# A two-layer decoder trunk in split float32 on one core: in W2's half products, the second plain block of the first column moved from ahead of the sixth product to between the second and the fourth

## The chip, the cores and the metric

One NeuronCore of one Trainium2 chip runs the whole kernel. The metric is the device time of one execution in microseconds (us), as the median of several runs. TensorE is called PE (its weight loads PEld), VectorE DVE, ScalarE ACT, GpSimd POOL, and SyncE SP; SP and POOL here mostly issue DMAs.

## The reference

A trunk of two layers over 256 tokens of width 2048: a gated-linear-attention layer, then a layer of sliding-window attention with sinks. Each ends with the MLP that takes most of the time, and that the change is in:

```python
def sqrelu_mlp(h, w1, w2):
    u = jax.nn.relu(h @ w1)        # 256 x 2048 by 2048 x 8192
    return (u * u) @ w2            # 256 x 8192 by 8192 x 2048
...
h = h + sqrelu_mlp(rmsnorm(h, norm_mlp[layer]), mlp_w1[layer], mlp_w2[layer])
```

All is float32.

## The kernel before

**Split float32.** Each float32 operand is held as a rounded high part and a rest (`wh`, `wl` for a weight). A product is then three matmuls: high by high, high by rest, rest by high. Weights come from HBM in blocks of 512 x 512 (a tile of 128 x 4 x 512, 1 MB). `halve` splits a block in two halves: for each, ACT casts 128 x 1024 to `wh` (line 124), then DVE subtracts to get `wl` (line 125). PE uses four slices of 128 rows of a block; each half holds two. There are four half tiles of `wh` in all (two blocks), three of `wl`, and three of `ws`, the tile into which plain blocks are loaded. A tile is refilled only when its last reader is done.

**W2 by sets of half products.** `seven` computes, for two of W2's four columns of 512 and one group g of 2048 of its rows, a 4 x 2 arrangement of blocks: rows 0 and 1 by a Strassen-like scheme of seven products, each for 128 tokens only (12 matmuls of 128 x 512), rows 2 and 3 by plain blocks for all 256 tokens (24 matmuls). Block (i, j) is row i, column j of the two. In each MLP, g goes from 0 to 3, and each g has two sets: n = 0 (columns 0 and 1; the "first set" below) and n = 1 (columns 2 and 3, the "second set"). That is 8 first and 8 second sets. For g over 0 two column pairs of W1 (`two_columns`) are computed ahead of the two sets, so the second sets of g = 0, 1, 2 are followed by W1.

I call the products by the index of their left operand (`op[0]` to `op[6]`); the change's name counts from one. A set runs, in the order of the code: product 0 into PSUM bank A; plain block (2,1) into banks E and F; product 2 into E; plain (3,1) into E and F; product 4 into D; product 6 into C; plain (2,0), then plain (3,0), into A and C; product 5 into D; product 1 into A; product 3 into C. Banks go on accumulating, and DVE reads them between: `x21 += D` after product 4 (line 1163), `x22 -= C` after product 6 (line 1164), `v += D` after product 5, `x11 += A` and `x21 += C` at the end. So a product that goes on in D waits until x21 has read D, and plain (2,0)'s second half, which goes on in C, waits until x22 has read C. `apart=True` puts plain (2,0)'s 12 matmuls for bank A ahead of its 12 for bank C.

**The shared block x.** `x` (tile `wx`) is loaded once a set and then changed in place: POOL's accumulating DMA adds block (0,1) after product 0, DVE adds `y` (tile `wy`, line 1212) after product 4, and block (1,0), called `b21` (lines 1223 to 1225), after product 5. Products 0, 4, 5 and 3 use its states. `b12` is block (0,1) plus y (line 1207), for product 6; the same sum for W1's columns is line 315, and W1's x is line 254 (POOL's accumulating DMA), 256 (its load), 330 (plus y).

**What sets the order.** A scheduler orders each engine's instructions when the program is built. `tc.high_priority(offset=WPRI)` lets loads, splits and sums of weights run ahead of other work. On the chip each engine then takes its own list in order, and waits on semaphores.

Of the kernel before, what the change touches and what calls it, by code (L numbers as in the profile page):

```python
# [21 lines left out]
C = 512  # L22
# [29 lines left out]
def yoco_kernel(ctx: ExitStack, tc: tile.TileContext, x, norms, mlp_w1, mlp_w2, a_w_in, w_glr, w_gate, a_g_o, a_w_o,  # L52
# [24 lines left out]
    def tick():  # L77
        now[0] += 1
        for fn in due.pop(now[0], ()):
            fn()  # L80

    def mm(o, l, r, start=True, stop=True, **kw):
        nc.tensor.matmul(o, lhsT=l, rhs=r, start=start, stop=stop, **kw)  # L83
# [23 lines left out]
    def halve(ws, o=C, n=2, gain=None):  # L107

        whs = [wp.tile([P, 2, C], F32R, name="wh", tag="wh", bufs=WHL) for _ in range(2)]
        wl = wp.tile([P, 4, C], F32R, name="wl", tag="wl", bufs=WS)  # L110
        with tc.high_priority(offset=WPRI):
            for k in range(0, 4, n):
                wh = whs[k // 2]
                js, ks = slice(k % 2, k % 2 + n), slice(k, k + n)
                w = ws[k // 2] if isinstance(ws, list) else ws[:, ks, :o]
                if gain is not None:
                    for j in range(k, k + n):
                        g = gain[:, j:j + 1]
                        h = wh[:, j % 2, :o]
                        nc.scalar.activation(out=h, in_=ws[:, j, :o], func=AF.Copy, scale=g)  # L120
                        nc.vector.scalar_tensor_tensor(out=wl[:, j, :o], in0=ws[:, j, :o], scalar=g, in1=h.bitcast(F32),
                                                       op0=ALU.mult, op1=ALU.subtract)
                    continue
                nc.scalar.copy(out=wh[:, js, :o], in_=w)  # L124
                nc.vector.tensor_sub(out=wl[:, ks, :o], in0=w, in1=wh.bitcast(F32)[:, js, :o])  # L125
        return [(whs[k // 2][:, k % 2], wl[:, k]) for k in range(4)]

    def split_w(parts, step=4, gain=None):
        ws = wp.tile([P, 4, C], F32, name="ws", tag="ws", bufs=WS)
        with tc.high_priority(offset=WPRI):  # L130
            for k in range(0, 4, step):
                ks = slice(k, k + step)
                o = 0
                for ap in parts:
                    n = ap.shape[1]
                    nc.sync.dma_start(out=ws[:, ks, o:o + n],
                                      in_=ap[k * P:(k + step) * P].rearrange("(k p) n -> p k n", p=P))
                    o += n
        return halve(ws, o, min(step, 2), gain)
# [826 lines left out]
    def mlp(w1, w2, act, r, gains):  # L966
# [141 lines left out]
        def seven(w, n, op, us, g, acts, gains, sq, nr):  # L1108
# [6 lines left out]
            def block(i, j):  # L1115
                return w[i * C:(i + 1) * C, (c0 + j) * C:(c0 + j + 1) * C]
# [13 lines left out]
            def use(b):  # L1130
                if b in banks:
                    return banks[b], False
                banks[b] = bank([P, C], "ms" if b in "EF" else "acc")
                return banks[b], True

            def product(b, o, ws):
                p, st = use(b)
                halves = halve(ws)
                for k in range(4):
                    wh, wl = halves[k]  # L1140
                    mm(p, op[o][:, 0, k], wh, st and k == 0, False, skip_group_check=True)
                    mm(p, op[o][:, 0, k], wl, False, False, skip_group_check=True)
                    mm(p, op[o][:, 1, k], wh, False, k == 3, skip_group_check=True)
                tick()
                return p

            def plain(i, j, b0, b1, apart=False):

                halves = split_w([block(i, j)])
                ah, al, _ = us[i]  # L1150
                ps_ = [use(b) for b in (b0, b1)]
                order = [(k, t) for k in range(4) for t in range(NT)]
                for n, (k, t) in enumerate(sorted(order, key=lambda kt: kt[1]) if apart else order):
                    wh, wl = halves[k]
                    p, st = ps_[t]
                    tt = slice(t * P, (t + 1) * P)
                    mm(p, ah[:, k, tt], wh, st and k == 0, False, skip_group_check=True)
                    mm(p, ah[:, k, tt], wl, False, False, skip_group_check=True)
                    mm(p, al[:, k, tt], wh, False, k == 3, skip_group_check=True)
                    if n % 4 == 3:  # L1160
                        tick()
# [48 lines left out]
            sub(x22, product("C", 6, b12))  # L1210
            with tc.high_priority(offset=WPRI):
                nc.vector.tensor_add(out=x, in0=x, in1=y)
            for i in (2, 3):
                plain(i, 0, "A", "C", i == 2)
            p = product("D", 5, x)
            with tc.high_priority(offset=WPRI):
                add(v, p)
# [6 lines left out]
            with tc.high_priority(offset=WPRI):  # L1224
                nc.vector.tensor_add(out=x, in0=x, in1=b21)
            product("A", 1, b21)
            add(x11, banks["A"])
            if g == n + 2 == 3 and not gains:

# [20 lines left out]
        for g in range(4):  # L1250
# [50 lines left out]
            for n in range(2):  # L1301
                seven(w, n, op, us, g, acts, gains, sq, nr)
# [242 lines left out]
```

## Time and profile before

| | |
|---|---|
| median of 3 runs | 2015.89 us (2015.86 to 2015.92) |
| the profiled execution | 2016.46 us, span of its instructions 2014.5 us |
| PE busy | 2000.6 us, 9714 matmuls |
| PEld, DVE, ACT busy | 1661.5, 1751.7, 1310.2 us |
| granted TensorE clock | 1.00 throughout |
| HBM | read 429.78 MB, written 6.29 MB |

The profile's rows give the line, engine, operation and tiles, a busy time, and in brackets how long the engine stood idle before, with what released it. A PE row's length is that of one pipelined matmul; the rate is read from the starts of successive rows.

### The profile page before, as it was taken

Reading aid. Unit: us, or ns where it says so; the run is one execution under the profiler, and the core shown is the slowest. Engines: PE = TensorE matmul, PEld = TensorE weight load, DVE = VectorE, ACT = ScalarE, POOL = GpSimd, SP = SyncE. Lnnn points to the kernel's source line nnn. Section 1 sums busy time; section 2 is a strip of 40 time slices with the busy share of each in tenths; the row PEclk is TensorE's granted clock in tenths of the full one; section 3 lists DMA queues with packets and bytes.
Section 4 is the critical chain, followed back from the end, with each engine's and each line's share of the span. In section 5 each row is a group of like instructions: output and inputs, shape, how many; then the busy total and the mean of one; then the engine's idle time right before and its main releaser. Section 6 shows DMA issues by size and latency. Waiting matters only on the chain.

```text
span 2014.5 us, 25811 instructions
## 1 busy us (share of the span) xinstructions
PE 2000.6 (99%) x9714; PEld 1661.5 (82%) x9714; DVE 1751.7 (87%) x1938; ACT 1310.2 (65%) x1740; POOL 180.7 (9%) x199
## 2 busy tenths in 40 slices
PE   9999999999999999999999999999999999999999
PEld 9998888888888888888888878788888888887887
DVE  6697787789889989989998676898889989988998
ACT  6746666667557657656766787666657656755765
POOL 1161110000000000000001121000000000000000
PEclk9999999999999999999999999999999999999999
DMA  8445775796787787778765443787687778778774
GB/s 288 147 157 177 209 230 189 193 297 198 231 266 224 222 266 231 229 252 254 203 205 183 163 132 124 208 286 208 222 264 228 234 247 254 207 228 263 223 224 127
DMA packets 220972, 437.74 MB, mean 217 GB/s; under 512 B 8000, under 2 KB 18512, under 8 KB 218800
## 3 DMA queue, kind: packets, MB, share of 16 engines
q1 hardware_dynamic: 195296, 380.92, 55.6%
q0 software_dynamic: 22464, 53.30, 14.0%
q10 hardware_dynamic: 3088, 1.88, 0.3%
q8 instruction: 76, 1.25, 0.2%
q14 instruction: 48, 0.39, 0.1%
HBM read 429.78 MB, written 6.29 MB: 216 GB/s over the span
## 4 chain that ended last, share of the span: by engine, by line
PE 90%; DVE 3%; ACT 2%; issue 2%; DMA 2%; POOL 0%; SPq 0%; ACTq 0%; POOLq 0%; DVEq 0%
PE acc L83 66%; PE ms L83 15%; PE tp L83 6%; PE tp L1013 1%; DMA wx<-in_mlp_w_dram 1%; DVE wl L125 1%; ACT sc L1428 1%; DMA ws<-in_a_w_in_dram 1%; PE tp L852 1%; DVE ws L315 0%; ACT wh L124 0%; PE tp L1359 0%; ACT wh L120 0%; DVE sc L1438 0%; PE tp L722 0%
## 5 line engine op out<-in xcount | busy, mean ns | idle before, releaser
L83 PE MATMUL acc<-wh,act 128*128 128x512 f32 x2928 | 939.1, 393 | 0.0
L124 ACT CAST wh<-ws 128x1024 fp32r<-128x1024 f32 x536 | 561.5, 1052 | 326.1 <-PE acc L83 199.1
L125 DVE TENSOR_TENSOR wl<-ws,wh 128x1024 fp32r<-128x1024 f32 x536 | 658.4, 1241 | 86.3 <-ACT wh L124 82.4
L83 PEld LDWEIGHTS acc<-wh,act 128*128 128x128 f32 x2928 | 548.1, 188 | 116.3 <-DVE xs L1164 2.6
L83 PE MATMUL acc<-wl,act 128*128 128x512 f32 x1464 | 570.4, 390 | 0.0
L124 ACT CAST wh<-wx 128x1024 fp32r<-128x1024 f32 x272 | 286.2, 1053 | 195.7 <-PE acc L83 141.4
L125 DVE TENSOR_TENSOR wl<-wx,wh 128x1024 fp32r<-128x1024 f32 x272 | 327.8, 1220 | 72.8 <-ACT wh L124 69.2
L83 PEld LDWEIGHTS acc<-wl,act 128*128 128x128 f32 x1464 | 275.2, 188 | 55.3 <-issue 1.2
L83 PE MATMUL ms<-wh,act 128*128 128x512 f32 x512 | 166.3, 393 | 0.0
L83 PE MATMUL acc<-act,wh 128*128 128x256 f32 (+1 forms) x640 | 141.5, 308 | 1.0 <-ACT wh L422 1.0
L83 PE MATMUL acc<-wh,op 128*128 128x512 f32 x384 | 123.4, 389 | 0.0
L83 PE MATMUL acc<-wh,ops 128*128 128x512 f32 (+1 forms) x392 | 123.1, 386 | 0.0
L83 PEld LDWEIGHTS ms<-wh,act 128*128 128x128 f32 x512 | 96.2, 188 | 19.5
L83 PEld LDWEIGHTS acc<-act,wh 128*128 128x128 f32 x640 | 104.5, 191 | 6.5 <-ACT wh L422 1.3
L83 PE MATMUL acc<-act,wl 128*128 128x256 f32 x384 | 107.7, 284 | 0.5 <-DVE wl L423 0.3
L83 PE MATMUL ms<-wl,act 128*128 128x512 f32 x256 | 99.7, 390 | 0.0
L83 PE MATMUL tp<-wh,cmb 128*128 128x512 f32 x288 | 94.6, 389 | 0.0
L83 PE MATMUL acc<-wh,cmb 128*128 128x512 f32 x264 | 85.9, 392 | 0.0
L83 PEld LDWEIGHTS acc<-wh,ops 128*128 128x128 f32 x392 | 73.1, 188 | 14.5
L83 PEld LDWEIGHTS acc<-wh,op 128*128 128x128 f32 x384 | 72.1, 188 | 15.0
L1126 POOL DMA_DIRECT2D wx<-in_mlp_w_dram x16 | 20.6, 1288 | 656.7 <-DVE wl L125 616.3
L83 PE MATMUL acc<-wl,ops 128*128 128x512 f32 (+1 forms) x196 | 76.2, 389 | 3.1 <-DVE wl L125 3.1
(306 smaller groups left out, 2666.6 us busy)
## 6 DMA issues: line engine op xcount, KB each, us to landing
ws<-in_mlp_w_dram SPq DMA_DIRECT2D x196, 1024.0 KB, 5.4
ws<-in_a_w_in_dram SPq DMA_DIRECT2D x42, 1024.0 KB, 5.0
wy<-in_mlp_w_dram SPq DMA_DIRECT2D x30, 1024.0 KB, 6.6
wx<-in_mlp_w_dram SPq DMA_DIRECT2D x16, 1024.0 KB, 5.3
wx<-in_mlp_w_dram POOLq DMA_DIRECT2D x16, 1024.0 KB, 9.4
ws<-in_b_w_q_dram SPq DMA_DIRECT2D x16, 1024.0 KB, 5.1
ws<-in_a_w_o_dram SPq DMA_DIRECT2D x15, 1024.0 KB, 5.1
ws<-in_b_w_o_dram SPq DMA_DIRECT2D x15, 1024.0 KB, 5.1
```

The source lines that it names most:

```text
L83: nc.tensor.matmul(o, lhsT=l, rhs=r, start=start, stop=stop, **kw)
L124: nc.scalar.copy(out=wh[:, js, :o], in_=w)
L125: nc.vector.tensor_sub(out=wl[:, ks, :o], in0=w, in1=wh.bitcast(F32)[:, js, :o])
L852: nc.tensor.transpose(out=tp[:, j, t], in_=xs[c][:, t, (2 * b + j) * P:(2 * b + j + 1) * P], identity=ident)
L1013: nc.tensor.transpose(out=tp[:, k, :], in_=h[:, k * P:(k + 1) * P], identity=ident)
L1126: nc.gpsimd.dma_start(out=ws, in_=block(i, j).rearrange("(k p) n -> p k n", p=P), accum_op=ALU.add)
L1428: nc.scalar.activation(out=sc[:, h], in_=sc[:, h], func=AF.Exp, bias=nmx[:, h:h + 1], scale=f[:, h:h + 1], accum_out=su[:, h:h + 1])
```

## The change

In every set, plain block (3,0) runs between product 1 and product 3 instead of ahead of product 5.

```diff
@@ -1210,8 +1210,7 @@
             sub(x22, product("C", 6, b12))
             with tc.high_priority(offset=WPRI):
                 nc.vector.tensor_add(out=x, in0=x, in1=y)
-            for i in (2, 3):
-                plain(i, 0, "A", "C", i == 2)
+            plain(2, 0, "A", "C", True)
             p = product("D", 5, x)
             with tc.high_priority(offset=WPRI):
                 add(v, p)
@@ -1224,6 +1223,7 @@
             with tc.high_priority(offset=WPRI):
                 nc.vector.tensor_add(out=x, in0=x, in1=b21)
             product("A", 1, b21)
+            plain(3, 0, "A", "C")
             add(x11, banks["A"])
             if g == n + 2 == 3 and not gains:
```

No instruction is added or removed. The orders are the scheduler's, so the text alone does not tell them.

PE, first set of the first MLP's g = 0, before: the end of plain (2,0)'s part for bank A (`acc_4523`), and then, before its part for bank C (`acc_4668`), the first matmuls of plain (3,0) (`wh_4725`):

```order
L83 MATMUL acc_4523<-wl_4694,act_4478 128x512
L83 MATMUL acc_4523<-wh_4693,act_4478 128x512
L83 MATMUL acc_4523<-wh_4725,act_4515 128x512
L83 MATMUL acc_4523<-wl_4727,act_4515 128x512
L83 MATMUL acc_4523<-wh_4725,act_4515 128x512 x2
L83 MATMUL acc_4523<-wl_4727,act_4515 128x512
L83 MATMUL acc_4668<-wh_4692,act_4478 128x512
```

The same place on PE now, where `acc_4647` is bank D and `op1_3728` the operand of product 5:

```order
L83 MATMUL acc_4523<-wl_4694,act_4478 128x512
L83 MATMUL acc_4523<-wh_4693,act_4478 128x512
L83 MATMUL acc_4647<-wh_4723,op1_3728 128x512
L83 MATMUL acc_4647<-wl_4725,op1_3728 128x512
L83 MATMUL acc_4647<-wh_4723,op1_3728 128x512 x2
```

Product 5 now follows plain (2,0)'s 12 matmuls for bank A at once; all its 12 run, then the first matmul of product 1, then plain (2,0)'s 12 for bank C. In the second sets only the first matmuls of product 5 (three in most) stand ahead of those 12.

DVE, same first set, before (`ws_4690` is plain (2,0), `ws_4723` plain (3,0), `wx_4521` x, `xs_2953<-acc_4647` the sum x21 += D):

```order
L125 TENSOR_TENSOR wl_4694<-ws_4690,wh_4693 128x1024
L125 TENSOR_TENSOR wl_4727<-ws_4723,wh_4725 128x1024
L125 TENSOR_TENSOR wl_4727<-ws_4723,wh_4726 128x1024
L1163 TENSOR_TENSOR xs_2953<-acc_4647,xs_2953 128x512
L1164 TENSOR_TENSOR xs_3029<-xs_3029,acc_4668 128x512
```

And now:

```order
L125 TENSOR_TENSOR wl_4694<-ws_4690,wh_4693 128x1024
L125 TENSOR_TENSOR wl_4725<-wx_4521,wh_4723 128x1024
L125 TENSOR_TENSOR wl_4725<-wx_4521,wh_4724 128x1024
L1163 TENSOR_TENSOR xs_2953<-acc_4647,xs_2953 128x512
L1224 TENSOR_TENSOR wx_4521<-wx_4521,ws_4743 128x2048
L1164 TENSOR_TENSOR xs_3029<-xs_3029,acc_4668 128x512
```

The two splits of x for product 5 stand where those of plain (3,0) stood, still ahead of the sum that frees bank D.

DVE, end of the second set of g = 0, before (`wx_4819` is x, `ws_5066` b21, `v1_3720` v, `ws_5204` the block of the next W1 columns that gets y added, `wx_5122` their first block):

```order
L1225 TENSOR_TENSOR wx_4819<-wx_4819,ws_5066 128x2048
L125 TENSOR_TENSOR wl_5071<-ws_5066,wh_5069 128x1024
L315 TENSOR_TENSOR ws_5204<-ws_5204,wy_5183 128x2048
L1163 TENSOR_TENSOR v1_3720<-acc_4937,v1_3720 128x512
L125 TENSOR_TENSOR wl_5071<-ws_5066,wh_5070 128x1024
L125 TENSOR_TENSOR wl_5091<-wx_4819,wh_5089 128x1024
```

And now (`ws_5033` is b21, `ws_5055` plain (3,0)):

```order
L1224 TENSOR_TENSOR wx_4819<-wx_4819,ws_5033 128x2048
L125 TENSOR_TENSOR wl_5038<-ws_5033,wh_5036 128x1024
L125 TENSOR_TENSOR wl_5038<-ws_5033,wh_5037 128x1024
L1163 TENSOR_TENSOR v1_3720<-acc_4937,v1_3720 128x512
L125 TENSOR_TENSOR wl_5059<-ws_5055,wh_5057 128x1024
L125 TENSOR_TENSOR wl_5059<-ws_5055,wh_5058 128x1024
L125 TENSOR_TENSOR wl_5091<-wx_4819,wh_5089 128x1024
L125 TENSOR_TENSOR wl_5091<-wx_4819,wh_5090 128x1024
L315 TENSOR_TENSOR ws_5204<-ws_5204,wy_5183 128x2048
L125 TENSOR_TENSOR wl_5128<-wx_5122,wh_5126 128x1024
```

Line 315's sum no longer stands between the two halves of b21 (product 1) but behind both halves of x for product 3. In the first sets the sum of line 1207 for the next set stands between the two halves of that set's product 0. The loads of b21 and plain (3,0) change places in SP's list.

## The prediction

> **What bounds the kernel now.** First the page's busy times and its chain of waits:
>
> ```profile
> span 2014.5 us, 25811 instructions
> PE 2000.6 (99%) x9714; PEld 1661.5 (82%) x9714; DVE 1751.7 (87%) x1938; ACT 1310.2 (65%) x1740; POOL 180.7 (9%) x199
> PE 90%; DVE 3%; ACT 2%; issue 2%; DMA 2%; POOL 0%; SPq 0%; ACTq 0%; POOLq 0%; DVEq 0%
> ```
>
> PE is the bound, and the change neither adds nor removes a matmul. So only PE's stalls count: who is waited for, in the view of waits, and where. PE's and PEld's own rows (total, times, longest):
>
> ```profile
> PEld acc L83 <- DVE wl L125: 5.6, 6, 0.9
> PEld acc L83 <- DVE xs L1164: 2.6, 15, 0.2
> PEld tp L83 <- DVE wl L125: 2.5, 6, 1.1
> PE acc L83 <- DVE wl L125: 3.1, 6, 0.5
> ```
>
> Six long waits for a `wl`, and six in another bank. The timeline shows the first of the six, in product 1 of a second set:
>
> ```profile
> 573.92 0.84 PE L83 MATMUL acc<-wh,ops 128*128 128x512 f32 x3
> 575.27 0.19 PEld L83 LDWEIGHTS acc<-wl,ops 128*128 128x128 f32 x1 [0.93 <-DVE wl L125]
> 575.27 0.50 PE L83 MATMUL acc<-wl,ops 128*128 128x512 f32 x1 [0.51 <-DVE wl L125]
> 575.61 0.62 PE L83 MATMUL acc<-wh,ops 128*128 128x512 f32 x2
> 567.86 2.29 DVE L1225 TENSOR_TENSOR wx<-wx,ws 128x2048 f32<-128x2048 f32 x1
> 570.07 1.22 DVE L125 TENSOR_TENSOR wl<-ws,wh 128x1024 fp32r<-128x1024 f32 x1
> 571.20 2.28 DVE L315 TENSOR_TENSOR ws<-ws,wy 128x2048 f32<-128x2048 f32 x1
> 573.40 0.69 DVE L1163 TENSOR_TENSOR v<-acc,v 128x512 f32<-128x512 f32 x1
> 574.00 1.22 DVE L125 TENSOR_TENSOR wl<-ws,wh 128x1024 fp32r<-128x1024 f32 x1
> ```
>
> A matmul is due 0.227 us after the one before (573.92 with three: the next at 574.60). It came at 575.27, 0.67 late, and its successor after 0.34 instead of 0.227, another 0.11: 0.78 us lost. DVE ends the missing `wl` at 575.22. It did line 1225, half of b21, line 315 and the sum into v without a break: four products in a row (5, 1, 3 and the next) leave it no slack for sums of 2.3 us.
>
> **The change part by part.** *The six stalls.* Now 24 matmuls of plain (3,0) stand behind product 1. Second set, on the trace's clock; ahead of product 5 nothing moves:
>
> ```profile
> 559.12 0.39 PE L83 MATMUL acc<-wh,act 128*128 128x512 f32 x1
> 558.83 0.69 DVE L1163 TENSOR_TENSOR xs<-acc,xs 128x512 f32<-128x512 f32 x1
> 559.43 2.35 DVE L125 TENSOR_TENSOR wl<-ws,wh 128x1024 fp32r<-128x1024 f32 x2
> 561.70 0.68 DVE L1164 TENSOR_TENSOR xs<-xs,acc 128x512 f32<-128x512 f32 x1
> ```
>
> Plain (2,0) starts at 559.12; after 12 matmuls (2.72) product 5 is due at 561.84. Its two splits take the place at 559.43; x21 has read bank D by 559.52. After three matmuls, at 562.52, plain (2,0)'s second half needs x22's sum: done at 562.38. It ends at 565.24, the rest of product 5 (9) at 567.28, product 1 at 570.0, plain (3,0) at 575.4, product 3 at 578.2. DVE: line 1224 562.3 to 564.6; b21's second cast can start when plain (2,0) has been read, at 565.4, is done 1.06 later, its `wl` 1.22 after that at 567.7. It is needed at the eighth matmul, 567.28 + 1.59 = 568.9. Stall gone: 6 x -0.78 = **-4.7 us** (bounds: 0 if something else is late there, -4.7).
>
> *A new wait in the first sets.* There x21 is not ahead of product 5's splits. The same place before:
>
> ```profile
> 518.26 0.39 PE L83 MATMUL acc<-wh,act 128*128 128x512 f32 x1
> 518.47 1.06 ACT L124 CAST wh<-ws 128x1024 fp32r<-128x1024 f32 x1 [0.31 <-DVE wl L125]
> 517.22 3.56 DVE L125 TENSOR_TENSOR wl<-ws,wh 128x1024 fp32r<-128x1024 f32 x3
> 520.70 0.68 DVE L1163 TENSOR_TENSOR xs<-acc,xs 128x512 f32<-128x512 f32 x1
> 521.30 0.68 DVE L1164 TENSOR_TENSOR xs<-xs,acc 128x512 f32<-128x512 f32 x1
> 522.03 0.19 PEld L83 LDWEIGHTS acc<-wh,act 128*128 128x128 f32 x1 [0.17 <-DVE xs L1164]
> ```
>
> Of the three splits in one row, the last two were plain (3,0)'s and are now product 5's; the last cannot come sooner, its cast ends at 519.53. So x21 += D still runs 520.70 to 521.38. Product 5 goes on in bank D, and is due at 518.26 + 12 x 0.227 = 520.98. It starts at 521.43, 0.45 late, and the restart costs 0.11 as above: 0.55. The wait at 522.03 goes (some 0.04; before, the first matmuls of plain (3,0) covered the sum for x22). Net 0.5 x 8 sets = **+4.0 us**. Bounds: 0 (the order of DVE excludes a gain) and 0.93 a set, the longest such wait above: +7.4. I take 0.5, since each term has its row.
>
> In these sets x22's sum now stands behind line 1224: 521.30 + 2.2 + 0.68 = 524.2. Plain (2,0)'s second half is due after product 5 and one matmul, 524.3. Free, by 0.1.
>
> By the Trainium skill, "TensorE: Matmul & The Clock Gate", Part 2 (what each phase is for), only weight loads are pulled ahead and matmuls keep their program order; by it the wait for D holds up everything behind and the term is +4.0, and if other matmuls could pass it, 0. The trace agrees with the rule: at 575.27 the matmuls by `wh` behind the late one, long ready, waited too.
>
> *W1's product 5 behind the second sets.* PE reaches it 0.8 us sooner per stall removed. The last of the six waits in `tp`, and the DMAs at the first place of the kind:
>
> ```profile
> 1851.52 1.05 ACT L124 CAST wh<-wx 128x1024 fp32r<-128x1024 f32 x1 [2.63 <-DMA wx<-in_mlp_w_dram]
> 1853.88 0.19 PEld L83 LDWEIGHTS tp<-wl,cmb 128*128 128x128 f32 x1 [1.07 <-DVE wl L125]
> 577.52 0.88 SPq L256 DMA_DIRECT2D wx<-in_mlp_w_dram  x2
> 578.93 2.46 POOL L254 DMA_DIRECT2D wx<-in_mlp_w_dram  x2 [7.85 <-DVE wl L125]
> DMA to landing us min/median/max: 5.9/7.8/11.8
> ```
>
> POOL's accumulating load of the second half of x lands 11.8 us after issue, among two SP loads issued a microsecond earlier. Of the 2.5 us that PEld waits there, each wait holds some 0.15 of the weight load's normal lead, so PE loses about 1.5. SP's two loads wait for x's splits for product 3, formerly done at 577.5, now at 572.9; POOL's wait for the first splits of the next columns and move by 1 us at most. With the rivals out of the way they land in less: 578.93's pair at 5.9 (the minimum) would be ready 4 us ahead. I take **-1.5 us** (bounds -1.5 and, if the landing doesn't move, +4.0: next part).
>
> *The end of the kernel.*
>
> ```profile
> 2007.35 0.60 PE L1172 MATMUL ms<-ident,xs 128*128 128x128 f32 x4
> 2007.41 1.01 DVE L1163 TENSOR_TENSOR xs<-acc,xs 128x512 f32<-128x512 f32 x2
> 2008.15 0.66 PE L1172 MATMUL tp<-ident,xs 128*128 128x128 f32 x4 [0.20 <-DVE xs L1163]
> ```
>
> The transposes of x11 wait for its sum, which stood behind several other DVE steps. Now these run under plain (3,0). 2007.35 + 4 x 0.11 = 2007.79 was due: **-0.4 us** (0 to -0.4).
>
> *At nothing.* Plain (3,0)'s load is issued 8 us later, b21's 8 sooner; a 1 MB load takes 5.4 (page row below) and is split 5 us after it lands. x11 is not read before the next group, except at the end. The first sets' delays shift all that follows alike.
>
> Sum: -4.7 + 4.0 - 1.5 - 0.4 = -2.6 us on the profiled 2016.46, whose span is 2014.5; the median 2015.89 is 0.57 below, so **2013.3 us**.
>
> **The rivals.** *B: product 5 doesn't wait in the first sets* (x21 a little sooner, or nothing lost at the bank). Against it: three rows fix 521.38. Time 2009.3, faster.
>
> *C: line 315 is late.* Its block's buffer is b21's now, so its load is issued at 567.7 (before: ahead of 562), among two loads of sums:
>
> ```profile
> 565.78 0.58 POOL L997 DMA_DIRECT2D cmb<-kept  x1 [27.05 <-PE acc L83]
> 570.54 0.54 POOL L997 DMA_DIRECT2D cmb<-kept  x1 [4.18 <-PE acc L83]
> ws<-in_mlp_w_dram SPq DMA_DIRECT2D x196, 1024.0 KB, 5.4
> cmb<-kept POOLq DMA_DIRECT2D x12, 1024.0 KB, 5.1
> ```
>
> At 5.4 it lands at 573.1, just as DVE has done the splits for product 3 (572.9). Behind it stand a sum and two splits (2.2, 1.14, 0.6 for x11, 1.22: 5.2) for the eighth matmul of the next product, due 578.2 + 1.6 = 579.8. So it may land up to 574.6, after 6.9; beyond, each us costs 6. At 7.6 us: +4.2, 2017.5. By the Trainium skill, "DMA: Bandwidth & Descriptors", Issuing engines are not separate DMA queues, all issuers' transfers interleave on the same 16 engines: that speaks for C, and against the change; the 11.8 us above agrees.
>
> *D: the gain is given back at W1's product 5*, the POOL load landing as late as now. Then of the -4.7 some 4.0 come back (two of the six waits have slack), and the 1.5 stays: -0.7 + 4.0 - 0.4 = +2.9, 2018.8. Against it: SP's loads move 4.6 us forward.
>
> *E, slower: line 1207 in the first sets.* It now stands ahead of the second split of the next product 0, and its block takes plain (3,0)'s buffer, free at 529.6. DVE reaches it at 535.3, behind x11's sum (bank A complete at 534.5). Sum and split need 3.4 us; the matmul is due at 539.3. So the load may take 6.3 us from issue; beyond, each us costs 8. At 7.1 us: +6.6, 2019.9, from there on slower. Against it: 5.4 as the median, and no sum's load beside it.
>
> **How the numbers follow.** 0.2% is 4.0 us, about what can be told from no change. Main case 0.50 (own range 2012.0 to 2014.8), B 0.18, C 0.12, D 0.10, E 0.10. Faster than 2011.9: B and a little of the main case's edge, 0.21. Slower than 2019.9: E and the tails of C and D, 0.11. The same: 0.68. The range 2009.0 to 2018.8 takes in B, and C and D up to their prices, and leaves out E and the tails.
>
> **What would show it.** Right: no `wl` wait over 0.5 us in product 1 of the second sets; eight PE waits for x21's sum (line 1163) at product 5 of the first sets, near 0.5 each; the POOL load of W1's x landing sooner, no 1.07 in `tp`; x11's transposes unbroken at the end. Wrong: PE waiting behind line 315 or 1207 for a DMA, or `tp` waits grown by 0.7.

## The result, and the profile after: slower by 0.7%

| | before | changed |
|---|---|---|
| median | 2015.91 us (4 runs, 2015.86 to 2016.15) | 2030.58 us (4 runs, 2028.04 to 2031.91) |
| ratio | | 1.0071, 95% interval 1.0059 to 1.0083 |
| profiled execution, span | 2016.46, 2014.5 us | 2029.25, 2027.2 us |

The forecast was 2013.3, with 2018.8 as its upper end: wrong by 17 us, and in sign. Single runs of the changed kernel spread over 4 us, those of before over 0.3.

The page's busy times and the rows of waits that changed, in the changed kernel:

```profile
span 2027.2 us, 25798 instructions
PE 2005.9 (99%) x9714; PEld 1661.9 (82%) x9714; DVE 1755.8 (87%) x1938; ACT 1310.6 (65%) x1740; POOL 180.6 (9%) x199
...
PEld acc L83 <- DVE xs L1164: 7.2, 7, 1.3
PEld acc L83 <- DVE wl L125: 6.1, 12, 1.0
PEld tp L83 <- DVE wl L125: 0.4, 2, 0.2
...
PE acc L83 <- DVE xs L1164: 4.4, 6, 0.9
PE acc L83 <- DVE xs L1163: 3.0, 8, 0.4
PE tp L852 <- DVE xs L1163: 2.1, 1, 2.1
...
DVE ws L315 <- DMA ws<-in_mlp_w_dram: 7.8, 4, 2.7
DVE gkq L1334 <- DMA gk<-in_b_g_q_dram: 4.1, 1, 4.1
DVE ws L1207 <- DMA ws<-in_mlp_w_dram: 2.0, 4, 0.6
```

`PE acc` for line 1163, eight times: the wait for x21 that was forecast. `tp` fell from 2.5 to 0.4: forecast too. New are six waits for line 1164 (x22's sum), one at the transposes of line 852, and DVE's waits for DMAs at lines 315, 1334 and 1207. The twelve PEld waits for a `wl` in `acc` are not those of product 1: seven stand in products 0 and 4, five behind line 315.

**The forecast wait.** First set, at product 5 (PE, then DVE):

```profile
520.36 0.39 PE L83 MATMUL acc<-wh,act 128*128 128x512 f32 x1
521.13 0.47 PE L83 MATMUL acc<-wh,op 128*128 128x512 f32 x1 [0.38 <-DVE xs L1163]
517.95 2.43 DVE L125 TENSOR_TENSOR wl<-wx,wh 128x1024 fp32r<-128x1024 f32 x2
520.30 0.68 DVE L1163 TENSOR_TENSOR xs<-acc,xs 128x512 f32<-128x512 f32 x1
```

Product 5 was due at 520.59 and came at 521.13, behind the sum of 520.30: 0.54, and 0.08 at the restart (the next starts 0.30 later). Eight times 0.62 is 5.0 us.

**The wait that was not forecast.** The second set that follows, from the end of the first set on. DVE, then POOL, then ACT; before:

```profile
533.65 3.49 DVE L125 TENSOR_TENSOR wl<-wx,wh 128x1024 fp32r<-128x1024 f32 x3
542.88 2.28 DVE L1207 TENSOR_TENSOR ws<-ws,wy 128x2048 f32<-128x2048 f32 x1
537.44 1.28 POOL L1126 DMA_DIRECT2D wx<-in_mlp_w_dram  x1 [40.10 <-DVE wl L125]
547.08 1.06 ACT L124 CAST wh<-wx 128x1024 fp32r<-128x1024 f32 x1 [0.30 <-PE ms L83]
```

and now, with PE and DVE at product 5 behind it:

```profile
534.63 0.69 DVE L1163 TENSOR_TENSOR xs<-acc,xs 128x512 f32<-128x512 f32 x1
535.23 2.28 DVE L1207 TENSOR_TENSOR ws<-ws,wy 128x2048 f32<-128x2048 f32 x1
537.43 1.22 DVE L125 TENSOR_TENSOR wl<-wx,wh 128x1024 fp32r<-128x1024 f32 x1
538.94 1.28 POOL L1126 DMA_DIRECT2D wx<-in_mlp_w_dram  x1 [42.04 <-DVE wl L125]
548.48 2.00 ACT L124 CAST wh<-wx 128x1024 fp32r<-128x1024 f32 x2 [1.43 <-DMA wx<-in_mlp_w_dram]
560.50 2.35 DVE L125 TENSOR_TENSOR wl<-wx,wh 128x1024 fp32r<-128x1024 f32 x2
562.77 0.68 DVE L1164 TENSOR_TENSOR xs<-xs,acc 128x512 f32<-128x512 f32 x1
562.57 0.39 PE L83 MATMUL acc<-wh,op 128*128 128x512 f32 x1
563.50 0.50 PE L83 MATMUL acc<-wh,act 128*128 128x512 f32 x1 [0.54 <-DVE xs L1164]
```

Read down: line 1207's sum now stands ahead of the split of x's second half (537.43); before, the sum came at 542.88, long after that split. POOL's load into x must wait for that split, and goes out at 538.94 instead of 537.44; PE itself is 0.28 later at this place, so 1.2 us are lost. It takes 9.4 us to land, and ACT, which had been waiting for PE (547.08), now waits for the load (548.48). From there DVE has work without a break until x22's sum, 0.8 us behind its old distance to PE; PE has three matmuls of product 5 to do and then stands, 0.70 and 0.11 at the restart. This happens behind six of the eight first sets, with 0.67 to 1.06 each: 5.4 + 6 x 0.11 = 6.1 us.

At four of the six places line 1207's sum also waits for its own load, by 0.35 to 0.65 us, as at the next one (DVE, then POOL):

```profile
704.57 2.29 DVE L1207 TENSOR_TENSOR ws<-ws,wy 128x2048 f32<-128x2048 f32 x1 [0.59 <-DMA ws<-in_mlp_w_dram]
708.29 1.28 POOL L1126 DMA_DIRECT2D wx<-in_mlp_w_dram  x1 [42.74 <-DVE wl L125]
```

There POOL's load goes out 1.6 us later against PE and not 1.2, and PE's wait for x22 is 0.89 to 1.06 and not 0.67 to 0.70. So a part of the lateness is line 1207's place, and a part the load that it waits for.

**The end of the first MLP.** DVE and PE, and the granted clock (PEclk, before the DMA share) in one microsecond after it:

```profile
1094.67 0.23 DVE L1334 SCALAR_TENSOR_TENSOR gkq<-gk 128x64 f32<-128x64 f32 x1 [4.12 <-DMA gk<-in_b_g_q_dram]
1097.46 0.68 DVE L1163 TENSOR_TENSOR xs<-acc,xs 128x512 f32<-128x512 f32 x1
1098.20 0.55 PE L852 MATMUL tp<-ident,xs 128*128 128x128 f32 x3 [2.07 <-DVE xs L1163]
1100.09 1.05 PE L83 MATMUL acc<-wh,act 128*128 128x512 f32 x2
1100.00:1101.00 1.00, 1.00 (x4) 0.72 (x3) 1.00 (x3) 1.00 (x3) 0.18 (x1) 0.50 1.05 410
```

x21's last sum (1097.46) has slipped behind line 1334, a tiny product of norm gains for the next layer that waits for its load. PE's transposes wait 2.2 us; then the clock is granted at 0.50 and seven matmuls start 0.43 us apart. Together 3.8 us. Neither e1 nor e2 below, which move the block in one kind of set only, has this wait.

The account of the two profiled executions: gone 4.7 (product 1), 1.5 (`tp`) and 0.1 (end of the kernel); come 5.0 (x21), 6.1 (x22), 1.5 (weights of products 0 and 4 in second sets, four places), 2.4 (line 315, below), 3.8 (line 1334). That is +12.5 against +12.7 of the spans.

### The profile page after: what moved, and what is told of

It reads as the page before. It is cut to its first block, busy times and chain, and to the rows that moved or that the text cites. A ratio compares the mean times of both kernels' runs of the same rounds, so it can differ in the third digit from the quotient of the medians.

```text
span 2027.2 us, 25798 instructions
## 1 busy us (share of the span) xinstructions
PE 2005.9 (99%) x9714; PEld 1661.9 (82%) x9714; DVE 1755.8 (87%) x1938; ACT 1310.6 (65%) x1740; POOL 180.6 (9%) x199
## 4 chain that ended last, share of the span: by engine, by line
PE 54%; issue 30%; DVE 8%; DMA 4%; ACT 3%; POOL 1%; ACTq 0%; POOLq 0%; DVEq 0%; SPq 0%
PE acc L83 42%; PE ms L83 6%; DVE wl L125 5%; PE tp L83 3%; DMA wx<-in_mlp_w_dram 2%; ACT sc L1428 1%; DMA ws<-in_a_w_in_dram 1%; DVE xs L1163 1%; DVE wx L1212 1%; ACT wh L124 1%; DMA ws<-in_mlp_w_dram 1%; POOL wx L254 1%; PE tp L1013 1%; PE tp L852 0%; PE tp L1359 0%
```

## The experiments

On the chips of these runs the kernel before had the same median (2015.8 to 2016.0), but single runs from 2014 to 2019, so the times below are good to some 2 us either way. "Gain" is against the changed kernel's 2030.58 unless said otherwise.

**e1: the move in second sets alone.**

```diff
-            plain(2, 0, "A", "C", True)
+            early = n == 0
+            for i in (2, 3) if early else (2,):
+                plain(i, 0, "A", "C", i == 2)
...
             product("A", 1, b21)
-            plain(3, 0, "A", "C")
+            if not early:
+                plain(3, 0, "A", "C")
```

> The move is made in the second sets (n = 1) only; the first sets keep the old order. Theory L (line 1207's sum now stands on DVE between the two halves of x of the next product 0, so POOL's accumulating load of x is issued 1.2 us later, lands after it is due, and DVE enters plain (2,0) of the second set 0.8 us late; x22's sum then stops PE): the first sets' old order takes line 1207 away from there, so the six waits on x22 (6.3 us together) and the eight waits on x21 (5.0) vanish, and the six old waits in product 1 stay away: 2015.9 - 4.7 - 1.5, plus up to 4 for line 315's load and up to 3.8 at the end of the first MLP if line 1334 still stands ahead of x21's last sum: 2010 to 2014 if it doesn't, 2014 to 2018 if it does. Rival S (the second set's own new order makes DVE late): the six waits on x22 stay, 6.3 more: 2016 to 2020, and the trace shows them.

2013.11 us (11 runs); to the kernel before 0.9986 (0.9977 to 0.9995). No wait for x22 over 0.2 us, no wait for a weight in product 1, and one wait for x21 (0.7, in the first MLP's last set). The second set's own order was not the cause. It is the fastest version that computes the reference.

**e2: the move in first sets alone** (`early = n == 1`).

> The move is made in the first sets (n = 0) only; the second sets keep the old order. Theory L: line 1207 still stands between the halves of x, so the second sets' x22 wait (0.85 each, behind the first matmuls of plain (3,0)) comes although their own order is the old one, the eight waits on x21 (0.62 each) are there, and the six in product 1 (0.78) stay: 2015.9 + 5.0 + about 5 = 2026. Rival S: no x22 waits: 2015.9 + 5.0 = 2021.

2028.42, ratio to before 1.0064 (1.0051 to 1.0078): theory L. PE's rows of waits:

```profile
PE acc L83 <- DVE xs L1164: 4.5, 6, 0.9
PE acc L83 <- DVE xs L1163: 3.0, 8, 0.4
```

The six waits for x22 stand in second sets whose own order is the old one. The time is 2.4 above the forecast: in the profiled execution the waits for x22 came to 6.1 and not about 5, products 0 and 4 lost 1.5, and W1's product 5 lost 1.1 more than before.

**e4: POOL's load of x in two halves**, in the changed kernel.

```diff
-                    nc.gpsimd.dma_start(out=ws, in_=..., accum_op=ALU.add)
+                    for k in (0, 2):
+                        nc.gpsimd.dma_start(out=ws[:, k:k + 2], in_=...[:, k:k + 2], accum_op=ALU.add)
```

> The changed kernel with POOL's accumulating load of x (line 1126) as two loads of half a block; the first may start when the first half of x has been split, 2.5 us before the second, and each moves half the bytes. Theory L: x is ready for product 4 in time, the six waits on x22 in second sets vanish with the waits for product 4's weights there: 6 to 7.5 us less, about 2023. Rival S (the set's own order): no change, 2029 to 2031.

2019.84, a gain of 10.7. POOL and ACT at the same place:

```profile
535.64 1.20 POOL L1127 DMA_DIRECT2D wx<-in_mlp_w_dram  x1 [38.25 <-DVE wl L125]
539.57 1.20 POOL L1127 DMA_DIRECT2D wx<-in_mlp_w_dram  x1 [2.73 <-DVE wl L125]
547.99 1.06 ACT L124 CAST wh<-wx 128x1024 fp32r<-128x1024 f32 x1 [0.30 <-PE ms L83]
```

Each half lands in some 6.2 us instead of 9.4 for the whole, ACT waits for PE again, and no wait for x22 over 0.2 us is left: line 1207 reached PE by way of this load, as theory L says. The gain is larger than expected. In the profiled execution it is 6.5: the trace has 6.1 from the waits for x22, 0.7 from products 0 and 4 and 1.9 from the end of the first MLP, less 1.8 that line 315 (below) cost more. That the other runs gained more I can't place.

**e3: x21 freed by ACT.** In first sets ACT copies bank D to a tile and x21's sum reads that.

```diff
-            add(x21, p)
+            e = mp.tile([P, C], F32, name="e4", tag="e")
+            with tc.high_priority(offset=WPRI):
+                nc.scalar.copy(out=e, in_=p)
+            add(x21, e)
```

> The changed kernel; in the first sets ACT copies bank D to a tile as soon as product 4 is done, and x21's sum reads the tile, so bank D is free about 5 us before product 5. Theory: the eight waits at product 5 vanish, 8 x 0.62 = 5.0 us less than the changed kernel: about 2025 from 2030. Rival: DVE's queue, not the bank, holds product 5 (its weights would be next to be late): less than 1.5 us gained, the wait then named for a weight split.

2027.62, a gain of 3.0 by the medians: neither, and not clear of noise (ratio to the kernel before 1.0044 to 1.0069, against 1.0059 to 1.0083 of the changed kernel). So it is the trace that tells. PEld's row, against 7 times in the changed kernel:

```profile
PEld acc L83 <- DVE xs L1164: 9.8, 15, 1.3
```

The eight waits at product 5 are gone, and eight new ones, 0.33 each and 0.11 at the restart, stand 13 matmuls later, ahead of plain (2,0)'s second half: x22's sum, which the prediction had called free by 0.1, was covered by the wait for x21.

**e7: line 1334 on POOL** (two small operations there, none on DVE).

> The changed kernel with line 1334's small product (a load of norm gains, awaited by DVE ahead of x21's last sum at the end of the first MLP) done by POOL in two operations. Theory: DVE's 4.1 us wait ahead of that sum goes, PE's 2.2 us wait at the transposes and the 7 to 8 matmuls of 0.427 us behind it with it: 3.8 us less than the changed kernel, about 2026.5. Rival: x21's last sum is late by itself (product 3 ends 5.4 us nearer the end), and at most 1 us is gained.

2026.63, a gain of 4.0 as the theory has it, though the interval (1.0042 to 1.0067 to the kernel before) touches that of the changed kernel; no wait at the transposes and no slow matmuls.

**Line 315: e5, e6, e9.** In the profiles of the changed kernel and of e1, e3, e4 its load lands 5.8 to 8.5 us after issue, where all loads of its kind have a median of 5.4. e1, DVE's row and the issue's landing times (the first is this load's):

```profile
575.49 2.29 DVE L315 TENSOR_TENSOR ws<-ws,wy 128x2048 f32<-128x2048 f32 x1 [3.42 <-issue]
DMA to landing us min/median/max: 8.4/9.5/10.6
```

PE loses nothing there up to 6.5 us, 0.2 to 0.3 at 6.8, 1.2 at 7.7 and 1.9 at 8.45: about one for one from 6.6 on. e1 still loses 3.8 so. e5 was to move the sums' first load out of the way:

```diff
-            for a, o in zip(pairs, kept):
+            for a, o in reversed(list(zip(pairs, kept))):
```

> The second sets alone are changed, and POOL's two loads of kept sums (line 997) are issued in the opposite order, so that the first of them starts some 5 us later, behind the load of line 315's block. Theory C (line 315's load shares the DMA engines with the sums' load; in the four profiles so far PE lost nothing up to 6.5 us from issue to landing, 0.22 at 6.8, 0.6 at 7.1, 1.15 at 7.7, 1.86 at 8.45): the load lands within 6.6 us at all six places, and what line 315 cost with the second sets alone (3.8 us in that profile) goes: 2009.5 to 2011. Rival: the loads behind it (two halves of x and the next block, issued 3 to 6 us later) make it late, not the sums: landings stay at 6.5 to 8.5, 2012 to 2014.

> The kernel before with the same opposite order of the two loads of sums and nothing else. Theory C: line 315's load lies 5 us ahead of its need there and waits for nothing: no gain from it, 2015.9 within 1 us (at most the 1.5 us of W1's product 5, if its POOL load lands sooner). Rival: the opposite order is worth its 2 to 4 us by itself: 2012 to 2014.

e5 2013.85 (0.9985, 0.9976 to 0.9994), e6 2016.16 (0.9999, 0.9991 to 1.0008). Inconclusive: the first of the two loads still went out 2.07 us ahead of line 315's, as in e1; why the edit left it there no row shows. e5 so repeats e1, and gives the same time. e9 takes the loads out and fills their tiles with zeros, so that it no longer computes the reference:

```diff
-                    nc.gpsimd.dma_start(out=a.bitcast(F32), in_=o)
+                    nc.gpsimd.memset(a.bitcast(F32), 0.0)
```

> The second sets alone are changed, and the two loads of kept sums (line 997, 1 MB each) are left out: POOL fills their tiles with zeros, so that W1's products 3, 5, 6 and 7 compute with zeros. Run e5 did not move the first of these loads (it was issued 2.07 us ahead of line 315's load, as before), so it could not tell. Theory C (line 315's load shares the DMA engines with the sums' loads): its landings come down from 6.5 to 8.5 us to 5.2 to 6.2 us, PE no longer waits behind line 315, 3 to 4 us less than with the second sets alone: 2009 to 2010.5. Rival: the loads issued 3 to 6 us after it (the next block and two halves of x) make it late: landings stay over 6.5 us, 2012 to 2014.

2009.83 (2009.48 to 2011.34). SP's issues of blocks from 562 to 573 us (count, size of one, median us to landing), in e1 and then in e9:

```profile
ws<-in_mlp_w_dram SPq DMA_DIRECT2D x2, 1024.0 KB, 9.5
```

```profile
ws<-in_mlp_w_dram SPq DMA_DIRECT2D x2, 1024.0 KB, 5.4
```

Line 315's loads land within 5.1 to 6.0 us, PE waits nowhere behind them, and the spread shrinks to 2 us: the sums' loads made them late. The Trainium skill, "DMA: Bandwidth & Descriptors", Issuing engines are not separate DMA queues, has it that transfers of all issuers interleave on the same 16 engines. The trace agrees: without POOL's loads, SP's two land in a median of 5.4 us and not 9.5.

**e8: three cures at once** (e4, e5's order, e7), first sets still changed.

> The changed kernel with all three: POOL's load of x in two halves, the opposite order of the loads of sums, line 1334's product on POOL. If the trace's account is whole, 2029.3 (the profiled execution) - 6.3 (x22) - 1.4 (weights of products 0 and 4 in second sets) - 2.4 (line 315) - 3.8 = 2015.3, with only the eight waits on x21 (5.0) left of what the change added. If something else was lost that the account doesn't see: 2018 or more.

The profiled execution took 2015.32, as the account says, with the eight waits for x21 left. But luck has a part in that: e5's order moved nothing here either (the sums' first load goes out 2.07 us ahead of line 315's), line 315 still cost 0.9, and this was the fastest of eleven. The median is 2018.38 (ratio to before 1.0010, 1.0002 to 1.0019), in the range of the other forecast, that something is lost which the account doesn't see. The 3 us between them stay open.

**e10, e11: line 315's sum on POOL**, in the kernel before and in e1.

```diff
-                nc.vector.tensor_add(out=b12, in0=b12, in1=self.y)
+                (nc.gpsimd if self.pool else nc.vector).tensor_add(out=b12, in0=b12, in1=self.y)
```

> The kernel before, no block moved; only line 315's sum, for the W1 columns that follow a second set, is done by POOL and not by DVE. Theory: the six stalls in product 1 come from that sum alone standing between b21's splits, so they vanish (-4.7), and with them up to 1.5 at W1's product 5; nothing of what the move adds comes: 2010 to 2012. Rival P: POOL's sum holds back POOL's accumulating load of x, or slows DVE while it runs, and W1's products wait instead: 2014 or more.

> The second sets alone are changed, and line 315's sum for the W1 columns behind them is done by POOL. Theory C: DVE no longer stands behind a load that lands 6.5 to 8.5 us after issue, so the 3 to 4 us that PE lost there go: 2009 to 2010.5, and the spread of single runs (2011.3 to 2015.8 with the second sets alone) gets narrower. Rival P: POOL's sum holds back the accumulating load of x behind it, W1's product 5 waits instead: 2012 to 2015.

2032.66 (1.0086, 1.0072 to 1.0099) and 2018.30 (1.0010, 1.0001 to 1.0019). In e10 rival P came, by its second half: POOL's sum slows DVE. In e11 it is the same, though neither of its two forecasts names that or reaches 2018: a split of x beside POOL's sum takes 4.1 to 4.4 us and not 1.22, and PE waits 1.1 to 1.4 at each of the six places. e10, POOL, DVE and PE:

```profile
567.28 5.02 POOL L315 TENSOR_TENSOR ws<-ws,wy 128x2048 f32<-128x2048 f32 x1 [0.93 <-DMA ws<-in_mlp_w_dram]
567.86 6.59 DVE L1226 TENSOR_TENSOR wx<-wx,ws 128x2048 f32<-128x2048 f32 x1
575.64 0.80 PE L83 MATMUL acc<-wl,ops 128*128 128x512 f32 x1 [2.46 <-DVE wl L125]
```

POOL's sum takes 5.0 us, and the DVE sum beside it, 2.29 elsewhere, 6.59: it ends when POOL's end and its own length have passed. So e10 can't say whether product 1's stalls would go with line 315 alone. By the Trainium skill, "SBUF — State Buffer", Who interferes with whom, a DVE instruction with two SBUF inputs contends with a GpSimd instruction that reads SBUF; the trace agrees (567.28 + 5.02 + 2.29 = 574.6; it ended at 574.45).

**e12: line 315's block loaded earlier**, in e1: its load stands ahead of plain block (2,1)'s and gets a buffer that is free sooner.

```diff
             self.load_x(0, 0, False)
+            if self.pre:
+                self.b12 = self.load(0, 1)
```

> The second sets alone are changed, and line 315's block is loaded ahead of plain block (2,1) of the same W1 columns, so that it gets plain (2,0)'s buffer, some 9 us sooner; DVE then does its sum between x += b21 and the splits of b21. Theory: no wait for the load any more, but b21's first split ends about 0.5 us after product 1 needs it: 0.5 + 0.11 at each of the six places, 2009.8 (run e9, no wait at line 315) + 3.7 = 2013.5, with a narrower spread than the second sets alone. Rival: b21's splits have more slack than that (they wait for ACT's casts anyway): 2010 to 2011.5.

2018.30 (1.0014, 1.0005 to 1.0023): above both forecasts. The sum (line 317 here) went ahead of both splits of b21, and still waits for its load:

```profile
DVE ws L317 <- DMA ws<-in_mlp_w_dram: 4.3, 4, 1.7
PEld acc L83 <- DVE wl L125: 9.1, 12, 2.0
```

Now what is late by it is product 1 itself, by 0.2 to 2.0 us at the six places.

## Why the prediction was wrong, point by point

- **The six stalls, -4.7: right.** None is left in the changed kernel.
- **x21 in the first sets, +4.0: right,** at the place, from the cause and in number; 0.62 each and not 0.5, so 5.0.
- **W1's product 5, -1.5: right** in size (`tp` 2.5 to 0.4) and reason: POOL's load of x's second half, which took 11.0 to 12.6 us at the six places, takes 7.4 to 10.7.
- **The end of the kernel, -0.4:** 0.37 went, 0.24 came between these transposes and product 3.
- **The step that failed: "ahead of product 5 nothing moves".** It was read off the second set's own rows, and x22's sum given 0.1 us of slack from the old clock; so the forecast has no term for a wait of plain (2,0)'s second half there, and the runs have 6.1 us. But the first set before it had been reordered too, and its line 1207 held up a load that the second set needs 10 us later. Rival E had the place (line 1207 between the halves of x) and asked only whether the sum's own load and the next weight would be late. The split behind it also releases POOL's load of x, which had 0.5 us to spare (landed at 546.55, wanted at 547.08), and at the other five places 0.3 at most: at two of them ACT waited for it even in the kernel before. Against this 1.2 to 1.6 us: six waits, 6.1 us, and the waits of product 4, 0.9 of the 1.5. With the second sets' order alone the waits are absent (e1), with the first sets' alone they are there (e2), and with the load in two halves they go (e4). No run put line 1207's sum alone back; that it is this sum rests on the rows above.
- **Rival C, 0.12, 2017.5: it came,** 2.4 us in the profiled execution. I allowed 6.9 us; 6.6 is what the rows gave. I took 5.4, the median of all such loads, though the rows quoted for C put a sums' load beside this one: the case with the contention was the likely one, and the median was mostly that of loads without it.
- **Rival E, 0.10, 2019.9: its condition came in part.** Line 1207's load took 6.0 to 6.3 us at the four places where its sum waited, against about 5 at the others. E allowed 6.3, counted to PE's next weight; but DVE was there 5.7 after issue (529.53 to 535.23 at the first place), and from then on each bit of lateness held POOL's load back too. (E's price at 7.1 is also 8 x 0.8 = 6.4, not 6.6.)
- **"x11 is not read before the next group, except at the end": incomplete.** The first MLP has an end too, where the sums of the last set, x21's too, meet the next layer's small work on DVE; line 1334 cost 3.8 us, more than any other term that came but two.
- **Rivals B and D did not come:** product 5 did wait, and W1's product 5 gave nothing back.

## What to carry to other kernels

When a block moves, follow each reordered instruction to everything that it releases, first of all the transfers that wait for it, and compare their landing with the moment at which they are wanted now. A wait of 0.5 us at a place with 0.1 us of slack behind it is a chain of such waits: cure one, and the next shows (e3). And price a transfer by the row that has the same neighbours, not by the median of its kind.

A move need not be made everywhere: in the second sets alone it gained 2.9 us, in the first sets alone it cost 12.

## What was not expected of the hardware

- A GpSimd sum of 128 x 2048 float32 takes 4.6 to 6.7 us against DVE's 2.29, and a DVE sum that runs into it stands until it is done (6.59).
- An accumulating load of 512 KB lands in some 6.2 us (e4), where one of 1 MB takes 9.2 to 10.4 (the changed kernel).
- After PE waits of 2.2 to 2.7 us the granted clock fell to 0.50 for some 3 us in some cases and not in others: once in the changed kernel and once in e3, after three of e10's six waits of 2.6 to 2.7, and not after e4's of 1.9. The Trainium skill, "TensorE: Matmul & The Clock Gate", Part 1 (what's actually happening), has a free-running window, which makes the moment of a clock change vary, and lets the clock drop after at least one idle window of some 3.4 us; the waits here were shorter, so the measurement decides.
